# Small experts one at a time on both column halves, three fixed experts, an earlier ranking and another order at the end, in a mixer and grouped MoE layer

## Chip, cores and metric

One core of one Trainium2 chip. The time is device microseconds of one execution; the median of three runs of the kernel before is 969.6 (968.34 to 973.13). The profile is of one further execution. PE is TensorE, DVE VectorE, ACT ScalarE, POOL GpSimd, SP SyncE.

## What is computed

The layer has 1024 tokens of 1024 numbers, a token mixer (input projection, short convolution, pooling, spatial gating, output projection, LayerNorm), and then a mixture of 32 experts of which each token takes two:

```
h = x * (1 + scale2) + shift2
probs = softmax(h @ w_router + b_router)           # 32 experts in 4 groups of 8
g_sel = argmax over groups of the sum of the two best probs in the group
top_p, top_i = two best experts of that group ; weights = top_p / top_p.sum()
y[token] += weight * ((silu(xb @ w_gate[e]) * (xb @ w_up[e])) @ w_down[e])
x = LayerNorm(alpha * x + gate2 * y)
```

w_gate and w_up of an expert are 1024x512, w_down 512x1024, all fp32: 6 MB an expert, 192 MB in all, each read once. The tokens of an expert are some 26 to 130.

## The kernel before

**Mixer and routing.** Up to about 358 us the mixer runs in tiles of 128 tokens. Its last loop (over t) projects a tile, normalises it (`residual`), stores the row that the experts gather (`hrow`) and the base of the result (`acc_d`, both in DRAM), and routes it in three groups of tiles (`route_pick`, `route_place`, `route_list`). After the last group `ids` holds, for each expert, the tokens in its slots.

**Experts.** A work item is one big expert (a block of up to 128 tokens) or a pair of small ones (64 tokens each). The first four experts (`FIXED`) are processed as they are numbered, so that their weights can be loaded before routing is known. The other 28 are ranked by their count (`rank_experts`, `place_experts`): the largest gets two blocks (`DOUBLE`), the next eleven one block, the last sixteen 64 slots each, in eight pairs. `perm` holds the ranking; SP reads it (`expert`) before it issues a load of a ranked expert. A loop for overflowing experts runs at the end as often as `trip_i` says; it runs no time here.

**Chunks.** An expert's weights come in six chunks of 1 MB (gate and up in two each, down in two) into a ring of `NR` = 18 buffers, which also holds the split parts. A big expert's chunk is split into two parts of lower precision, wh (ACT, `split_tile`, L648) and wl (DVE, L653), and multiplied in three matmuls: wh with x_hi, wl with x_hi, wh with x_lo. A "whole" expert (the first one, and all small ones) is multiplied unsplit in fp32; each such matmul shows as two records in the trace. In a pair, the first expert's tokens are the 64 left stationary columns and the second's the 64 right ones, and each streams its own 512 weight columns (L1179, L1187).

**Order of work.** `chunks` lists the loads: up parts of an item, then the down parts of the item before. `Flow` counts buffers: `fill` issues loads while buffers are free, `take` splits, `parts_gone` frees the chunk that was used, takes ahead by `lead` chunks and fills up. A load is tied to the last matmul that has gone (`flow.last`). Every engine runs its instructions in the written order. `gather` fetches a block's rows into one of three buffers `xg` (POOL), `turn_part` transposes them, `swiglu` and `turn_h` make the hidden rows, `give` scales the output rows (L1232) and adds them to `acc_d` by an indirect accumulating DMA (L1234, POOL): one for a big block, two for a pair, 64 rows each. Scatters follow one another. Before the first block, three matmuls without use (`keep_warm`, L897) run on PE; the ranking and the sorting of the lists are small steps between the first two items' chunks (`steps_between`).

**End.** The last item is a pair; the down parts of a big expert and then of the pair come last. Then `acc_d` is read back and normalised (L1373 to L1405).

Of the kernel before, what the change touches and what calls it, by code (L numbers as in the profile page):

```python
# [38 lines left out]
AHEAD, FADE = 9, 12  # L39


@with_exitstack
def hybrid_trunk(ctx: ExitStack, tc: tile.TileContext, x, c, w_ada, b_ada, w_in, conv_w, conv_b,
# [48 lines left out]
    def load_rows():  # L92
        for r0, v in ((0, b_ada[0:2 * D].rearrange("(b p) -> b p", p=P)), (16, conv_w.rearrange("j (b p) -> (j b) p", p=P)),
# [25 lines left out]
                   allow_small_or_imprecise_dtypes=True)  # L119
    rcnt = const.tile([P, 2, 16], F32, name="rcnt")  # L120
# [23 lines left out]
    pw = const.tile([P, 2, P], F32, name="pw")  # L144
    nc.gpsimd.memset(pw, 0.0)
    wr = const.tile([P, KD, NE], F32, name="wr")
    br = const.tile([P, NE], F32, name="br")
    sgu = rt([P, 9, P], "sgu")
    wst, bs = sgu[:, 0:6], sgu[:, 6:9]
# [429 lines left out]

    xres = {}  # L580
# [5 lines left out]

    FIXED, BIG, DOUBLE, HALF = 4, 16, 4, P // 2
    PAIRS = (NE - BIG) // 2  # L590
    items = [(n,) for n in range(FIXED)]
    rest = [n for n in range(FIXED, BIG) if n != DOUBLE]
    rest.insert(1, DOUBLE)
    pairs = [(BIG + 2 * j, BIG + 2 * j + 1) for j in range(PAIRS)]
    for kind in "PBPBB" * 3 + "BPBBP":
        items.append((rest.pop(0),) if kind == "B" else pairs.pop(0))
# [10 lines left out]
    chunks, part_of = [], []  # L607
    for m in range(len(items) + 1):
        steps_ = [(w, h, m) for h in range(2) for w in (w_gate, w_up)] if m < len(items) else []
        steps_ += [(w_down, h, m - 1) for h in range(2)] if m else []  # L610
        for w, h, i in steps_:
            part = 1 + part_of[-1] if part_of else 0
            chunks += [(w, n, h) for n in items[i]]
            part_of += [part] * len(items[i])

    WHOLE = {items[0][0]} | set(range(BIG, NE))
    split_needed = [n not in WHOLE for _, n, _ in chunks]
# [243 lines left out]
    class Flow:  # L861
        taken, gone, used, others, lead, last = 0, 0, 0, 0, 2, None
# [18 lines left out]
    def parts_gone(last, n):  # L881
        flow.last = last
        for i in range(flow.gone, flow.gone + n):
            ready.pop(0)
            flow.used -= 1 + split_needed[i]
        flow.gone += n
        now = part_of[flow.gone] if flow.gone < len(chunks) else 0
        while (flow.taken < len(loaded) and part_of[flow.taken] - now < flow.lead and
               (not split_needed[flow.taken] or slots_used() + 1 < NR)):
            ready.append(take())  # L890
        fill(2)
# [6 lines left out]

    load_x(0)
    load_x(1)  # L900
    for t in range(NT):
# [32 lines left out]
        if t == NT - 1:  # L934

            flow.others = 3
# [5 lines left out]
    flow.others = 1  # L942
# [496 lines left out]
```

## Time and profile before

| | |
|---|---|
| median of 3 runs | 969.6 us |
| profiled execution | 968.15 us, its span 966.3 us |
| PE busy | 852.5 us (88%), 3992 instructions |
| DVE busy | 562.3 us (58%) |
| ACT busy | 364.3 us (38%) |
| POOL busy | 148.3 us (15%) |
| queue of loads (q1) | 258.25 MB, 68.3% of 16 DMA engines |
| software queue (q0: gathers, scatters, stores by POOL) | 26.60 MB, 9.7% |

The span is the time from the first to the last instruction of the profiled execution. Busy shares are means over the whole span; the stages have different limits, so they are read from windows. A matmul's end is modelled, so its duration overlaps the next one's; how fast matmuls follow each other is read from their starts.

### The profile page before, as it was taken

Reading aid. Unit: us, or ns where it says so; the run is one execution under the profiler, and the core shown is the slowest. Engines: PE = TensorE matmul, PEld = TensorE weight load, DVE = VectorE, ACT = ScalarE, POOL = GpSimd, SP = SyncE. Lnnn points to the kernel's source line nnn. Section 1 sums busy time; section 2 is a strip of 40 time slices with the busy share of each in tenths; the row PEclk is TensorE's granted clock in tenths of the full one; section 3 lists DMA queues with packets and bytes.
Section 4 is the critical chain, followed back from the end, with each engine's and each line's share of the span. In section 5 each row is a group of like instructions: output and inputs, shape, how many; then the busy total and the mean of one; then the engine's idle time right before and its main releaser. Section 6 shows DMA issues by size and latency. Waiting matters only on the chain. (4 is left out here: it accounts for less than half of the span.)

```text
span 966.3 us, 10876 instructions
## 1 busy us (share of the span) xinstructions
PE 852.5 (88%) x3992; PEld 584.2 (60%) x3992; DVE 562.3 (58%) x722; ACT 364.3 (38%) x401; POOL 148.3 (15%) x140
## 2 busy tenths in 40 slices
PE   3899999999799875999999999998999899899810
PEld 2778878877688752577555675565462657366400
DVE  6746844786667764687527356276170767266218
ACT  3453121124232333465515325065150655244207
POOL 0100000000000324222122131221211113111010
PEclk9999999999899997999999999999999999899975
DMA  9865163643444487189999999999999999999837
GB/s 302 286 211 227 71 191 109 218 153 111 194 174 153 166 320 312 44 323 377 417 404 414 398 366 393 394 416 407 391 409 396 412 402 384 381 382 413 330 93 279
DMA packets 77519, 285.58 MB, mean 296 GB/s; under 512 B 9852, under 2 KB 38856, under 8 KB 50840
## 3 DMA queue, kind: packets, MB, share of 16 engines
q1 hardware_dynamic: 66080, 258.25, 68.3%
q0 software_dynamic: 11296, 26.60, 9.7%
q8 instruction: 32, 0.52, 0.2%
q14 instruction: 23, 0.19, 0.1%
q10 hardware_dynamic: 88, 0.02, 0.0%
HBM read 268.79 MB, written 28.10 MB: 307 GB/s over the span
## 5 line engine op out<-in xcount | busy, mean ns | idle before, releaser
L653 DVE TENSOR_TENSOR wl<-w_raw,wh 128x2048 fp32r<-128x2048 f32 x90 | 204.4, 2288 | 109.4 <-ACT wh L648 104.9
L648 ACT ACTIVATE wh<-w_raw 128x2048 fp32r<-128x2048 f32 x90 | 171.1, 1914 | 108.8 <-DMA w_raw<-in_w_down_dram 65.4
L1179 PE MATMUL gu_ps<-w_raw,x_t 128*64 128x512 f32 (+1 forms) x544 | 139.8, 609 | 5.2 <-DMA w_raw<-in_w_up_dram 3.7
L1164 PE MATMUL gu_ps<-wh,x_hi 128*128 128x512 f32 x256 | 105.1, 410 | 0.0
L1165 PE MATMUL gu_ps<-wl,x_hi 128*128 128x512 f32 x256 | 100.8, 394 | 4.0 <-DVE wl L653 4.0
L1166 PE MATMUL gu_ps<-wh,x_lo 128*128 128x512 f32 x256 | 100.6, 393 | 0.0
L1179 PEld LDWEIGHTS gu_ps<-w_raw,x_t 128*64 128x64 f32 (+1 forms) x544 | 42.9, 142 | 79.0 <-issue 65.7
L295 PE MATMUL z_ps<-hh,w_hi 128*128 128x512 f32 x224 | 90.2, 403 | 0.0
L297 PE MATMUL z_ps<-hh,w_lo 128*128 128x512 f32 x224 | 87.3, 390 | 0.0
L296 PE MATMUL z_ps<-hl,w_hi 128*128 128x512 f32 x224 | 87.2, 389 | 0.0
L1187 PE MATMUL d_ps<-w_raw,m_ht 128*64 128x512 f32 (+1 forms) x272 | 63.8, 595 | 0.0
L1165 PEld LDWEIGHTS gu_ps<-wl,x_hi 128*128 128x128 f32 x256 | 48.2, 188 | 15.6 <-DVE wl L653 6.9
L1234 POOL DMA_INDIRECT acc_d<-m_o,place_ids x12 | 29.9, 2491 | 176.4 <-DVE m_o L1232 146.3
L1221 PE MATMUL d_ps<-wl,m_hl 128*128 128x512 f32 x128 | 51.7, 404 | 5.5 <-DVE wl L653 5.5
L669 PE MATMUL o_ps<-woh,y_lo 128*128 128x512 f32 x128 | 51.8, 404 | 5.4 <-DVE y_lo L466 5.4
L1220 PE MATMUL d_ps<-wh,m_hl 128*128 128x512 f32 x128 | 51.9, 405 | 4.3 <-ACT wh L648 4.3
L1164 PEld LDWEIGHTS gu_ps<-wh,x_hi 128*128 128x128 f32 x256 | 48.4, 189 | 12.0 <-issue 2.7
L1166 PEld LDWEIGHTS gu_ps<-wh,x_lo 128*128 128x128 f32 x256 | 48.1, 188 | 10.4
L667 PE MATMUL o_ps<-woh,y_hi 128*128 128x512 f32 x128 | 53.6, 419 | 0.0
L668 PE MATMUL o_ps<-wol,y_hi 128*128 128x512 f32 x128 | 51.5, 402 | 0.0
L1222 PE MATMUL d_ps<-wh,m_hl 128*128 128x512 f32 x128 | 51.1, 399 | 0.0
L295 PEld LDWEIGHTS z_ps<-hh,w_hi 128*128 128x128 f32 x224 | 42.1, 188 | 9.9 <-issue 1.4
(288 smaller groups left out, 1246.5 us busy)
## 6 DMA issues: line engine op xcount, KB each, us to landing
w_raw<-in_w_gate_dram SPq DMA_DIRECT2D x64, 1024.0 KB
w_raw<-in_w_up_dram SPq DMA_DIRECT2D x64, 1024.0 KB
w_raw<-in_w_down_dram SPq DMA_DIRECT2D x64, 1024.0 KB
ada_w<-in_w_ada_dram SPq DMA_DIRECT2D x16, 1024.0 KB
ada_w<-in_w_ada_dram SPq DMA_DIRECT2D x16, 512.0 KB
w_in<-in_w_in_dram SPq DMA_DIRECT2D x14, 512.0 KB
x_q<-in_x_dram SPq DMA_DIRECT2D x8, 512.0 KB
wo_raw<-in_w_out_dram SPq DMA_DIRECT2D x8, 512.0 KB
```

The lines of the kernel that those rows point to most:

```text
L295: nc.tensor.matmul(ps[:, h], wh, rhh, start=k == 0, stop=False)
L296: nc.tensor.matmul(ps[:, h], wh, rhl, start=False, stop=False)
L297: nc.tensor.matmul(ps[:, h], wl, rhh, start=False, stop=k == KD - 1)
L648: nc.scalar.activation(wh, w, AF.Copy)
L653: nc.vector.tensor_sub(wl, w, wh.bitcast(F32))
L667: nc.tensor.matmul(ps[:, h], hi[:, k], wh, start=k == 0, stop=False)
L1164: nc.tensor.matmul(ps[:, m], hi[:, k], wh[:, o], start=k == 0, stop=False)
L1165: nc.tensor.matmul(ps[:, m], hi[:, k], wl[:, o], start=False, stop=False)
L1166: last = nc.tensor.matmul(ps[:, m], lo[:, k], wh[:, o], start=False, stop=k == KD - 1)
L1179: last = nc.tensor.matmul(ps[sl, m], xt[:, k, sl], w[:, o], start=k == 0, stop=k == KD - 1)
L1187: last = nc.tensor.matmul(ps[sl, h], ht[:, k, sl], w[:, o], start=k == 0, stop=k == KF - 1)
L1220: nc.tensor.matmul(ps[:, h], hi[:, k], wh[:, o], start=k == 0, stop=False)
```

## The change

It has four parts. (1) Three experts are fixed instead of four, and none of them is whole. Of the first one, three chunks are split before routing ends: ACT makes three wh ahead of the token lists; the three wl, the ranking and the placing stand between the gather's issue and the first block. Tie-breaking constants are made earlier. 14 chunks are loaded before that instead of 18. (2) Small experts are items of their own: the same 64 tokens stand in both column halves, the left half streams 256 of a chunk's 512 columns, the right half the other 256; in the down part the halves stream the two halves of the 1024 output columns. The output has 64 rows of each half and is added with one scatter of 128 half rows. (3) The items come as B B B, S S, then B S alternating thirteen times, then S (B big, S small). (4) Before the last item, the down part of the item before it is loaded and used ahead of the last item's up part.

```diff
+FIXED, BIG, DOUBLE, HALF = 3, 16, 3, P // 2
+SMALL = NE - BIG
...
-    for kind in "PBPBB" * 3 + "BPBBP":
-        items.append((rest.pop(0),) if kind == "B" else pairs.pop(0))
+    rest.insert(3, DOUBLE)
+    for kind in "SS" + "BS" * 13 + "S":
+        items.append((rest if kind == "B" else small_).pop(0))
...
+        up = [(w, items[m], h) for h in range(2) for w in (w_gate, w_up)] if m < len(items) else []
+        dn = [(w_down, items[m - 1], h) for h in range(2)] if m else []
+        chunks += dn + up if m == len(items) - 1 else up + dn
-    WHOLE = {items[0][0]} | set(range(BIG, NE))
-    split_needed = [n not in WHOLE for _, n, _ in chunks]
+    split_needed = [n < BIG for _, n, _ in chunks]
...
-            flow.others = 3
+            flow.others = 3 + FIRST + 1
...
+    nc.scalar.activation(xg[2], g2row, AF.Copy, scale=0.0)
+    flow.others = 0
+    first = [take(True) for _ in range(FIRST)]
+    for g in xg[:2]:
         nc.scalar.activation(g, g2row, AF.Copy, scale=0.0)
     route_place(GROUPS[-1])
     route_list(GROUPS[-1])
...
-    def gate_up_whole(e, ps, k, m, parts):
-        xt, = xs[e]
+    def gate_up_half(e, ps, k, m, part):
+        xt = xs[e]
+        w, = part
         for k in range(k, k + 4):
-            o = slice((k % 4) * 512, (k % 4 + 1) * 512)
-            for sl, (w,) in columns(parts):
-                last = nc.tensor.matmul(ps[sl, m], xt[:, k, sl], w[:, o], start=k == 0, stop=k == KD - 1)
+            cols = by_row(w[:, (k % 4) * 512:(k % 4 + 1) * 512], KF)
+            for i, sl in enumerate(SIDES):
+                last = nc.tensor.matmul(ps[sl, m, 0:2 * P].rearrange("q (a p) -> q a p", a=2), xt[:, k],
+                                        cols[:, 2 * i:2 * i + 2], start=k == 0, stop=k == KD - 1)
+    def down_half(ht, ps, i, part):
+        w, = part
+        for a in range(2):
+            for j, sl in enumerate(SIDES):
+                last = nc.tensor.matmul(ps[sl, 0], ht[:, a, SIDES[i]], w[:, a * D + j * 512:a * D + j * 512 + 512],
+                                        start=a + i == 0, stop=a + i == 2)
...
+    def give_half(ps, n):
+        o = qt([P, D // 2], "m_o")
+        nc.vector.scalar_tensor_tensor(o, ps[:, 0], half_wts[:, n:n + 1], g2half, op0=OP.mult, op1=OP.mult)
+        add_rows(o, half_ids[:, n:n + 1], acc_d.rearrange("s (h n) -> (s h) n", h=2))
...
-    gather(upper_ids[:, 0:1], xg[2])
-    keep_warm(3)
+    gather(nothing, xg[2])
+    ranks, lists = rank_counts(), []
+    keep_warm(1)
     gather_to(3)
+    first[0][1]()
+    ranks = rank_experts(*ranks)
+    first[1][1]()
+    place_experts(*ranks)
+    keep_warm(1)
+    first[2][1]()
     for g in range(2):
         turn_blocks(0, g)
-    ready += [take() for _ in range(2)]
+    ready += [w for w, _ in first]
+    fill(0)
...
+        if not nxt:
+            flow.lead = 4
+            down(done, [turn_h(b) for b in done])
+        for i in range(4):
+            gate_up(i)
+            small_step(i)
+            if i == 0 and m and nxt:
+                turned = [turn_h(b) for b in done]
+            if i in (1, 2) and nxt:
+                turn_blocks(m + 1, i - 1)
+        gather_to(sum(b[0] <= m + 1 for b in seq) + 3)
```

`first[i][1]()` is the wl subtraction of a chunk whose wh is made already; `cols` takes every fourth column of a chunk's row (two interleaved sets for each half), so that the hidden rows fit the layout of w_down.

The instructions move at three places. First DVE between the cast of `ids` and the first block. Before, the ranking starts at once behind the cast (key, rank, onto, diag are its steps):

```order
L845 CAST ids<-ids_f 128x32
L996 COPY ranking<-cnt_ps 128x32
L998 SCALAR_TENSOR_TENSOR ranking<-ranking 128x32
L1000 MEMSET ranking 128x1 x4
L1002 SCALAR_TENSOR_TENSOR k_keyc<-cnt_ps,tie_c 32x1
L1003 SCALAR_TENSOR_TENSOR k_keyc<-eid_c,k_keyc 32x1
L1005 TENSOR_SCALAR k_own<-eid_c 32x1
L1007 TENSOR_SCALAR k_top<-eid_c 32x1
L1008 SCALAR_TENSOR_TENSOR k_keyc<-k_own,k_top,k_keyc 32x1
L1011 SCALAR_TENSOR_TENSOR ranking,k_rank<-ranking,k_keyc,ones 32x32
```

Now, from the last steps of the ranking to the first block's x_lo (one more wl, of the first chunk, stands right behind the cast):

```order
L1012 TENSOR_SCALAR ranking<-ranking,col 32x32
L1013 TENSOR_SCALAR ranking<-ident,k_rank 32x32
L663 TENSOR_TENSOR wl<-w_raw,wh 128x2048
L1020 CAST perm<-perm_ps 128x32
L1022 TENSOR_SCALAR o_at<-perm_ps 128x1
L1024 TENSOR_SCALAR left<-perm_ps 128x32
L1026 TENSOR_SCALAR ranking<-perm_ps 128x32
L1027 SCALAR_TENSOR_TENSOR left<-left,ranking 128x32
L1028 TENSOR_TENSOR left<-ranking,left 128x32
L663 TENSOR_TENSOR wl<-w_raw,wh 128x2048
L1148 TENSOR_TENSOR x_lo<-xg_ps,x_hi 128x512 x2
```

Three wl, the ranking and the placing now stand ahead of the x_lo of the first block; before, the first block had no x_lo.

Second PE in the middle of the expert stage. Before, a pair's up parts between two big experts (mh_ps transposes h, xg_ps the next block):

```order
L1179 MATMUL gu_ps<-w_raw,x_t 64x512 x8
L1203 MATMUL mh_ps<-ident,m_gh 128x128 x4
L1179 MATMUL gu_ps<-w_raw,x_t 64x512 x8
L1151 MATMUL xg_ps<-ident,xg_2682 128x128 x4
L1179 MATMUL gu_ps<-w_raw,x_t 64x512 x8
```

Now, a small expert behind a big one, with the down part of the small one before it ahead:

```order
L1178 MATMUL d_ps<-w_raw,m_ht 64x512 x8
L1170 MATMUL gu_ps<-w_raw,x_t 64x256 x8
L1202 MATMUL mh_ps<-ident,m_gh 128x128 x4
L1170 MATMUL gu_ps<-w_raw,x_t 64x256 x8
L1144 MATMUL xg_ps<-ident,xg_2684 128x128 x4
L1170 MATMUL gu_ps<-w_raw,x_t 64x256 x8
```

A chunk of one expert is now eight matmuls of 256 columns; before, two chunks of two experts were eight of 512.

Third PE at the end, up to the read of `trip_i`. Before, the last pair's up parts are followed by 24 matmuls of a big expert's down part, of which the first three stand here, with the pair's h transposed in their middle, and then by 16 matmuls of the pair's down part (L1187):

```order
L1179 MATMUL gu_ps<-w_raw,x_t 64x512 x8
L1203 MATMUL mh_ps<-ident,m_gh 128x128 x4
L1179 MATMUL gu_ps<-w_raw,x_t 64x512 x24
L1220 MATMUL d_ps<-wh,m_hl 128x512
L1221 MATMUL d_ps<-wl,m_hl 128x512
L1222 MATMUL d_ps<-wh,m_hl 128x512
```

Now:

```order
L1217 MATMUL d_ps<-wh,m_hl 128x512
L1197 MATMUL mh_ps<-ident,m_gh 128x128 x2
L1178 MATMUL d_ps<-w_raw,m_ht 64x512 x8
L1170 MATMUL gu_ps<-w_raw,x_t 64x256 x32
L1197 MATMUL mh_ps<-ident,m_gh 128x128 x2
L1178 MATMUL d_ps<-w_raw,m_ht 64x512 x8
```

The last eight chunks are those of small experts, unsplit, and the last down part is of one expert.

## Rows read from the trace of the kernel before

**Rows 1.** The page's strip of moved GB/s, in 40 slices of 24.2 us

```profile
GB/s 302 286 211 227 71 191 109 218 153 111 194 174 153 166 320 312 44 323 377 417 404 414 398 366 393 394 416 407 391 409 396 412 402 384 381 382 413 330 93 279
```

**Rows 2.** Stretches: length, busy time of each engine, granted clock, DMA share, GB/s

```profile
382.00:407.00 25.00, 22.67 (x78) 12.63 (x78) 14.75 (x38) 10.69 (x10) 10.18 (x15) 1.00 0.06 15
407.00:422.00 15.00, 15.00 (x58) 9.39 (x56) 7.73 (x21) 5.79 (x6) 0.10 (x1) 1.00 0.95 377
422.00:427.00 5.00, 5.00 (x26) 4.17 (x25) 4.97 (x3) 4.40 (x4) 0.00 (x0) 1.00 0.40 107
430.00:911.00 481.00, 458.06 (x2056) 283.24 (x2054) 251.88 (x170) 201.13 (x169) 97.01 (x50) 0.99 1.01 397
911.00:923.00 12.00, 10.65 (x49) 4.87 (x48) 2.63 (x4) 0.60 (x1) 1.57 (x1) 1.00 0.39 123
923.00:936.00 13.00, 0.00 (x0) 0.00 (x0) 1.12 (x1) 0.00 (x0) 2.98 (x2) 0.70 0.16 21
936.00:966.30 30.30, 0.00 (x0) 0.00 (x0) 22.65 (x29) 19.61 (x37) 0.00 (x0) 0.50 0.73 278
```

**Rows 3.** Timeline of SP around the gap in the loads: start, duration, instruction

```profile
364.20 0.33 SPq L637 DMA_DIRECT2D w_raw<-in_w_up_dram  x1
407.28 0.33 SPq L637 DMA_DIRECT2D w_raw<-in_w_gate_dram  x1
```

**Rows 4.** Timeline of PE and DVE, from the token lists to the first items

```profile
375.40 4.37 PE L897 MATMUL warm_ps<-g2row,ident 128*128 128x512 f32 x6
375.90 0.18 DVE L845 CAST ids<-ids_f 128x32 int32<-128x32 f32 x1
382.32 3.70 PE L1179 MATMUL gu_ps<-w_raw,x_t 128*128 128x512 f32 x8 [0.24 <-issue]
386.18 0.19 DVE L996 COPY ranking<-cnt_ps 128x32 f32<-128x32 f32 x1 [10.10 <-PE gu_ps L1179]
388.31 0.22 DVE L1015 TENSOR_SCALAR ranking<-ident,k_rank 32x32 f32<-32x32 f32 x1
389.87 2.29 DVE L653 TENSOR_TENSOR wl<-w_raw,wh 128x2048 fp32r<-128x2048 f32 x1 [1.34 <-issue]
408.48 0.69 DVE L1157 TENSOR_TENSOR x_lo<-xg_ps,x_hi 128x512 fp32r<-128x512 f32 x1 [0.80 <-ACT x_hi L1153]
```

**Rows 5.** Timeline of PE: two big experts, then a pair

```profile
424.16 0.63 PE L1203 MATMUL mh_ps<-ident,m_gh 128*128 128x128 f32 x4
441.97 0.63 PE L1203 MATMUL mh_ps<-ident,m_gh 128*128 128x128 f32 x4
457.15 3.65 PE L1179 MATMUL gu_ps<-w_raw,x_t 128*64 128x512 f32 x16
460.74 0.75 PE L1203 MATMUL mh_ps<-ident,m_gh 128*128 128x128 f32 x4
461.42 3.65 PE L1179 MATMUL gu_ps<-w_raw,x_t 128*64 128x512 f32 x16
491.52 7.09 PE L1187 MATMUL d_ps<-w_raw,m_ht 128*64 128x512 f32 x32
```

**Rows 6.** Timeline of PE in the mixer, and groups of weight loads by line and shape

```profile
195.43 1.97 PE L376 MATMUL mix_ps<-sgu,vn 128*64 128x128 f32 x32
L1151 PEld LDWEIGHTS xg_ps<-ident,xg 128*128 128x128 f32 x200 | 27.8, 191 | 21.5 <-issue 12.8 <-DVE m_hl L1211 3.3 <-DVE x_lo L1157 2.9
L355 PEld LDWEIGHTS v_ps<-ident,v 128*128 128x128 f32 x24 | 3.1, 140 | 1.3 <-ACT v L448 0.2 <-ACT vn L361 0.2
```

**Rows 7.** Timeline of DVE, POOL and SP at the end of the expert stage

```profile
922.83 1.28 DVE L1232 SCALAR_TENSOR_TENSOR m_o<-d_ps,pair_wts,g2row 128x1024 f32<-128x1024 f32 x1 [5.75 <-PE d_ps L1187]
924.39 1.42 POOL L1234 DMA_INDIRECT acc_d<-m_o,pair_ids  x1 [5.46 <-DVEq L1350]
928.94 1.56 POOL L1234 DMA_INDIRECT acc_d<-m_o,upper_ids  x1 [3.12 <-DMA acc_d<-m_o,pair_ids]
935.98 4.93 SPq L1373 DMA_DIRECT2D z<-acc_d  x8
```

More of the change, by code (lines that the diff above doesn't have):

```diff
@@ L578, in hybrid_trunk @@
         split_wo(k)
+    tie_breaks()
     xres = {}
@@ L879, in fill, with chunk_gone @@
             load_chunk(queue)
-    def parts_gone(last, n):
+    def chunk_gone(last):
         flow.last = last
[L883 to L888, printed above, removed]
+        ready.pop(0)
+        flow.used -= 1 + split_needed[flow.gone]
+        flow.gone += 1
+        while (flow.taken < len(loaded) and flow.taken - flow.gone < flow.lead and
                (not split_needed[flow.taken] or slots_used() + 1 < NR)):
@@ L1142, in turn_part @@
     def turn_part(e, src, g):
[L1144 removed]
+        if is_half(e):
+            if g == 0:
+                xt = xs[e] = qt([P, KD, HALF], "x_t")
+                ps = tp("xg_ps")
+                for j in range(KD):
+                    nc.tensor.transpose(ps[:, j * HALF:(j + 1) * HALF], by_row(src, KD)[0:HALF, j], ident[0:HALF, 0:HALF])
+                nc.scalar.activation(xt.rearrange("p a b -> p (a b)"), ps, AF.Copy)
+            return
         if g == 0:
[L1146 to L1147 removed]
+            xs[e] = qt([P, KD, P], "x_hi", F32R), qt([P, KD, P], "x_lo", F32R)
         hi = xs[e][0]
@@ L1299, in gate_up, with down @@
                     swiglu(b, p)
-            parts_gone(last, len(parts))
-        def down(blocks, turned, between=None):
-            it = items[blocks[0][0]]
-            whole = is_whole(blocks[0])
+            chunk_gone(last)
+        def down(blocks, turned):
             po = [zp("d_ps") for _ in blocks]
+            half = is_half(blocks[0])
             for i in range(2):
-                parts = ready[:len(it)]
                 for p, v in zip(po, turned):
-                    last = down_whole(v, p, i, parts) if whole else down_part(v, p, i, parts[0])
-                if i == 0 and between:
-                    between()
-                parts_gone(last, len(parts))
+                    last = (down_half if half else down_part)(v, p, i, ready[0])
+                chunk_gone(last)
             for b, p in zip(blocks, po):
-                give(p, weights(b), scattered(b))
+                if half:
+                    give_half(p, items[b[0]] - BIG)
+                else:
+                    give(p, weights(b), slots(b))
         def small_step(i):
```

218 lines of the change are left out of this document (82 added, 136 removed).

## The prediction

> **What bounds the kernel now.** I read the page's strip of bandwidth first [rows 1]: from slice 18 of 40 on, the DMA engines move some 400 GB/s in nearly every slice, with one hole (44 GB/s) at about 386 to 411 us and a fall at the end. So I cut the expert stage into stretches [rows 2]. Between 430 and 911 us the DMA share is 1.01 at 397 GB/s while PE is busy 458 of 481 us: DMA sets the pace, PE is close behind. Ahead of it lies the hole: 25 us (382 to 407) at 15 GB/s, later 5 us at 107 GB/s. Behind it come 12 us in which PE finishes, 13 us in which only the last scatters run, and 30.3 us of final LayerNorm. Three things can therefore change the time: when the stream of weights resumes, how long its bytes take, and what follows the last byte. The queue of loads [rows 3] says why the hole is there: the 18th load is issued at 364.20, the next at 407.28. All 18 buffers hold raw chunks, and each fixed expert behind the first needs a net buffer more for its split, so the buffers that the first expert frees go to splits and not to loads.
>
> **Part 1: three first chunks split early, ranking in the gap, three fixed experts.** By the order, only 14 chunks are loaded before the first block, a 15th once the first split is done, and the 16th once the third chunk has been used; from there each chunk used admits one load. The first block now waits on VectorE: behind the cast of `ids`, which ends at 376.1 [rows 4], stand three wl subtractions (2.29 each, 6.9), the ranking (2.35 from the first row to the last in the old form, of which seven small operations go: 1.6 left), the placing (six operations of some 0.2: 1.2), and x_lo (0.69): 386.5. In the kernel before, the first matmul ran at 382.32 and no x_lo was needed. From 386.5 ten of a chunk's twelve matmuls end the first chunk at 389.0 (a chunk takes 2.97, see below). Two warm-up matmuls stand where three stood, with waits between; in the old stretch a warm-up record took 0.73 us (4.37 over 6) against 0.46 in the block behind it (3.70 over 8) [rows 4], so the first chunk may run partly at the lower of the two clocks: up to 2.5 us more. I take 390; the ends are 385 (nothing waited for) and 394.
>
> A big expert takes PE 17.8 us, from one transposition of h (424.16) to the next (441.97) [rows 5], 2.97 a chunk. The third chunk is thus used at 396, and the 16th load goes out then, 11 us before the old 19th. Three loads fewer are in by that time, 3 x 1.0486 MB at 397 GB/s, 7.9 us: the net gain here is some 3 us, plus the second dip (5 us at 107 GB/s lose 3.7).
>
> **Part 2: bytes.** By 430 us some 24 loads had landed before (18, and 5.7 + 0.5 MB of the two stretches behind 407 [rows 2] with the first microseconds of the next), so the 191.0 MB of 430 to 911 (481 x 397) are 168 loads, 176.2 MB, and 14.8 MB of gathers and scatters. Rows whose index is out of bounds are not moved, so 64-row gathers and half-row scatters carry the same bytes. From 396 on there remain 177 loads and some 16.3 MB of indirect traffic: 201.9 MB, at 397 GB/s 508.6 us, so 904.6. In the first three experts loads are let in one per 2.97 us, near the pace of the stream itself (2.64 for a load alone at 397 GB/s), and the lists are still sorted there; I add 3 us: last weights at **908** (before 911).
>
> **Part 3: small experts.** Before, a pair's gate and up parts take 3.59 us for 16 records (8 matmuls, two records each: 457.15 to 460.74), 0.224 a record of 512 columns, and its down 7.09 for 32 [rows 5]. Now a chunk of one expert is again 16 records of 64 stationary columns, of 256 moving ones. The nearest rows: 32 records of the same halves with 128 columns take 1.97 us, 0.062 each [rows 6], and 0.224 at 512; between them 0.116 at 256, 1.86 a chunk. So a small expert costs 4 x 1.86, its down 3.55 (half of 7.09) and three groups of transpositions among half-array matmuls at 0.68 (460.74 to 461.42): 13.0 us. PE in all: 17 blocks x 17.8 and 16 x 13.0, 511 us, from 387 (390 less one chunk) to 898, against weights until 908. DMA stays the bound, with only 10 us to spare.
>
> One thing about these matmuls the trace does not show: their moving operand steps by 4 elements (16 bytes). The nearest row is a load of stationary columns: 128 of them with a step of 8 elements (xg_ps) take 191 ns, contiguous ones (v_ps) 140 [rows 6], 51 ns dearer. Nothing excludes a gain, but no row promises one, so the low end is 0; at the high end the same 0.4 ns a column falls on every moving column, 102 ns on each record of 116. I take 0: a half's stream asks for a column only every 0.88 ns (2 x 0.224 us for 512), twice the 0.4 ns that the step added to a loaded one, so it should fit into the pace. [...]
>
> **Part 4: the end.** Before, from 911 on: a split, half of a big expert's down, a pair's down, the output op at 922.83, two scatters of which the second waits for the first (924.39, 928.94), the reads at 935.98 [rows 7]: 25 us. Now the last eight chunks are unsplit ones of two small experts, one scatter follows. From 908: one down chunk 1.8, the output op on half the columns 0.7 (of 1.28), 0.3 to POOL, the scatter between 4.55 (first to second) and 7.04 (second to the reads), I take 5.8: **916.6**; the LayerNorm's 30.3 us [rows 2] give a span of 947. The last ln2 loads stay where they were in the queue.
>
> **What else moves, at no cost.** The tie breaks (POOL and four tiny VectorE operations) stand ahead of the projection, off any wait; the pair shift goes away; the pool weights in another buffer change nothing that waits. POOL issues as many scatters (33) and eight more gathers; it sat idle 384 us of 481 [rows 2]. If that cover went (a gather behind a scatter that waits), the next block's transpositions would be late by a scatter, some 5 us.
>
> **The sum.** Part 1 and 2: 911 to 908. Part 4: 25 us to 8.6. Span 966.3 to 947. The profiled run took 968.15 with a span of 966.3, so 1.85 lie around it, and the median of the runs is 969.6, 1.45 above it: 947 + 1.85 + 1.45 = **950 us**.
>
> **Rivals.**
> *Strided columns make PE the bound (slower).* If the step costs half of its high end, 51 ns a record, a gate or up chunk takes 2.67 and a small expert 16.3; PE needs 302.6 + 260 = 563 us, from 387 to 950, the span is 950 + 0.7 + 0.3 + 5.8 + 30.3 = 987, the time **990**; at the full 102 ns it is 1042, and so too if the two halves did not run side by side. It decides from 30 ns a record on: then PE ends at 929 and the span is the old one. For it: the 191 against 140 ns, and the thin spare. Against: the pace argument, and that halves of 128 columns do overlap [rows 6]. Chance 0.20.
> *VectorE becomes the bound in the first three experts.* Six splits (13.7), two x_lo, m_hl, m_gh at 0.69 and the output 1.28 come to 17.8 us an expert, just PE's 17.8, and now all three are split and the lists are sorted there. If PE loses 8 us, loads are let in that much later: **958**. For it: five microseconds at 422 to 427 had VectorE busy 4.97 [rows 2]. Against: three splits are done ahead. Chance 0.14.
> *Small experts stall between their chunks.* Their chunks are half as long, so the transposed blocks (two PSUM buffers, emptied by ScalarE and VectorE behind splits of 1.9 and 2.29 us) may come late. At 1.8 us an expert PE ends at 927, the span is 963: **967**, no change. For it: four transpositions between half-array chunks already take 0.68. Against: PE has 10 us to spare before any of it counts. Chance 0.08.
>
> **How the numbers follow.** The forecast, within 6 us of 950, has 0.58. A measurement of this kernel can tell about 0.5% (5 us) from no change. Faster by over that: forecast and second rival, 0.72; same 0.08; slower 0.20. The range: 944 (first chunk at 385, a scatter of 4.55) to 980, which takes in the second and third rivals and a step cost of up to 42 ns; what is left out above is most of the slower cases, below little.
>
> **What would show it.** In the changed profile the first third matmul of a block (wh with x_lo) should run near 386.5; the load behind the 15th near 396; GB/s from there near 397 without a hole; records of 64x256 every 0.116 us; PE idle some 10 us in the stage; last weights near 908; one scatter, reads at about 917. It would be wrong if gate/up chunks of small experts took over 2.3 us, if DMA fell under 385 GB/s for long with PE full, or if the first block started after 394.

## The result and the profile after

The changed kernel takes **1071.2 us** (median of 4 runs, 1069.4 to 1075.4) where the kernel before took 969.1 beside it (4 runs): a ratio of 1.105, 95% interval 1.1003 to 1.1097. I had forecast 950, with 944 to 980 as the range. The profiled execution took 1069.4 with a span of 1067.6.

The page's strip of bandwidth of the changed kernel (26.7 us a slice; before: [rows 1]):

```profile
GB/s 304 229 275 122 188 50 197 182 134 217 177 139 208 285 92 264 333 399 310 348 363 338 295 262 204 382 308 324 344 353 343 367 359 322 376 346 334 306 35 291
```

Before, it stood at some 400 from slice 19 to 37. Now it lies mostly between 300 and 360: the DMA no longer sets the pace. The same in stretches (length, busy time of PE, PEld, DVE, ACT, POOL, then granted clock, DMA share, GB/s), to hold against [rows 2]:

```profile
366.00:380.00 14.00, 7.97 (x36) 4.29 (x37) 13.41 (x54) 6.93 (x6) 7.59 (x4) 0.50 0.14 33
380.00:396.00 16.00, 12.18 (x43) 9.17 (x42) 8.13 (x11) 8.23 (x8) 11.55 (x14) 0.71 0.28 96
411.00:430.00 19.00, 18.88 (x78) 15.10 (x77) 11.24 (x20) 10.13 (x8) 2.38 (x3) 0.85 0.67 231
445.00:980.50 535.50, 534.75 (x2421) 304.35 (x2420) 247.22 (x175) 192.72 (x175) 92.12 (x54) 1.00 0.93 334
1006.50:1036.70 30.20, 22.18 (x98) 7.32 (x98) 3.02 (x4) 1.15 (x3) 4.69 (x3) 0.97 0.26 70
```

From 445 to 980 PE is busy 534.75 of 535.5 us, and the DMA has fallen to 334 GB/s. PE is the bound. The hole in the loads has not gone but moved ahead (33 GB/s from 366 to 380, 96 from 380 to 396, since 14 chunks are in and not 18), only 231 GB/s flow between 411 and 430, and PE still has 22 us of work and the scatters another 8 behind 1006.5. What PE does, in its timeline around one small expert and the down of the one before it (start, duration, instruction):

```profile
578.00 3.65 PE L1178 MATMUL d_ps<-w_raw,m_ht 128*64 128x512 f32 x16
581.49 3.80 PE L1170 MATMUL gu_ps<-w_raw,x_t 128*64 128x256 f32 x16
585.22 0.74 PE L1202 MATMUL mh_ps<-ident,m_gh 128*128 128x128 f32 x4
```

Held against the pair of [rows 5]: the down of one small expert takes 3.49 us (578.00 to 581.49), half of the pair's 7.09, as forecast. A gate or up chunk takes 3.73 (581.49 to 585.22), though its records have half the columns of the pair's, which took 3.59. That is 0.233 us a record where I had put 0.116. There are 64 such chunks: 64 x (3.73 - 1.86) = 120 us more on PE.

The start of the stage, PE (what it waited for stands in brackets) and VectorE, to hold against [rows 4]:

```profile
381.40 0.79 PE L1157 MATMUL gu_ps<-wh,x_lo 128*128 128x512 f32 x1
388.83 0.40 PE L1055 MATMUL ls_ps<-ranking 32*128 32x32 f32 x2 [1.43 <-DVE ranking L1047]
391.62 0.60 PE L1056 MATMUL ls_ps<-ranking 32*128 32x16 f32 x2 [2.39 <-DVE ranking L1053]
410.81 0.37 PE L1045 MATMUL lt_ps<-ident,ranking 128*32 128x128 f32 x1 [4.11 <-DVE ranking L1277]
412.26 0.63 PE L1156 MATMUL gu_ps<-wl,x_hi 128*128 128x512 f32 x1
412.68 0.63 PE L1157 MATMUL gu_ps<-wh,x_lo 128*128 128x512 f32 x1
```

```profile
371.81 0.18 DVE L855 CAST ids<-ids_f 128x32 int32<-128x32 f32 x1
386.29 2.29 DVE L663 TENSOR_TENSOR wl<-w_raw,wh 128x2048 fp32r<-128x2048 f32 x1 [4.35 <-ACT wh L658]
388.50 0.27 DVE L1047 COPY ranking<-lt_ps 32x128 f32<-32x128 f32 x1
389.15 2.29 DVE L663 TENSOR_TENSOR wl<-w_raw,wh 128x2048 fp32r<-128x2048 f32 x1 [0.37 <-ACT wh L658]
391.36 0.21 DVE L1053 COPY ranking<-ranking 32x128 f32<-32x128 f32 x1
408.29 2.28 DVE L663 TENSOR_TENSOR wl<-w_raw,wh 128x2048 fp32r<-128x2048 f32 x1
410.48 0.18 DVE L1277 COPY ranking<-tab 128x32 f32<-128x32 f32 x1
```

This execution reached the lists some 4 us earlier than the profiled one of before (`ids` cast at 371.81 against 375.90). From the end of that cast (371.99) to the first matmul with x_lo (381.40) it took 9.4 us; I had forecast 10.4. Then comes what I had allowed 3 us for: the list steps need matmuls on PE, whose inputs are tiny VectorE copies, and these copies stand in VectorE's queue behind wl subtractions of 2.29 us, the first of which had itself waited 4.35 us for ScalarE's wh. PE waits 1.43, 2.39 and 4.11 us for the copies. After the last of these its records come 0.42 us apart (412.26, 412.68): the granted clock was 0.50 from 412 to 416, and also from 392 to 396, behind the second wait.

### The profile page after: what moved, and what is told of

The parts are those of the page before. It is cut to its first block, busy times and chain, and to the rows that moved or that the text cites. A ratio compares the mean times of both kernels' runs of the same rounds, so it can differ in the third digit from the quotient of the medians.

```text
span 1067.6 us, 12238 instructions
## 1 busy us (share of the span) xinstructions
PE 976.6 (91%) x4590; PEld 635.0 (59%) x4590; DVE 583.6 (55%) x738; ACT 376.4 (35%) x425; POOL 160.2 (15%) x150
## 3 DMA queue, kind: packets, MB, share of 16 engines
q0 software_dynamic: 11936, 26.60, 9.4%
## 4 chain that ended last, share of the span: by engine, by line
PE 81%; DVE 9%; another core or an unknown queue 3%; ACT 2%; DMA 2%; issue 1%; SPq 0%; DVEq 0%; ACTq 0%; POOLq 0%
PE gu_ps L1170 21%; PE gu_ps L1155 6%; PE gu_ps L1156 6%; PE gu_ps L1157 6%; PE z_ps L315 5%; PE z_ps L316 5%; PE z_ps L317 5%; PE d_ps L1178 4%; PE d_ps L1215 3%; PE d_ps L1216 3%; PE d_ps L1217 3%; PE xg_ps L1144 2%; PE o_ps L677 2%; PE o_ps L679 2%; PE o_ps L678 2%
## 5 line engine op out<-in xcount | busy, mean ns | idle before, releaser
L663 DVE TENSOR_TENSOR wl<-w_raw,wh 128x2048 fp32r<-128x2048 f32 x96 | 217.9, 2289 | 64.1 <-ACT wh L658 59.9
L1170 PE MATMUL gu_ps<-w_raw,x_t 128*64 128x256 f32 x1024 | 243.0, 632 | 0.0
L658 ACT ACTIVATE wh<-w_raw 128x2048 fp32r<-128x2048 f32 x96 | 179.4, 1906 | 14.1 <-PE gu_ps L1156 8.5
L1170 PEld LDWEIGHTS gu_ps<-w_raw,x_t 128*64 128x64 f32 x1024 | 75.1, 150 | 129.3 <-issue 124.3
L1157 PE MATMUL gu_ps<-wh,x_lo 128*128 128x512 f32 x272 | 108.1, 398 | 0.0
L1189 DVE TENSOR_TENSOR m_gh<-m_gh,gu_ps 128x512 f32<-128x512 f32 (+1 forms) x33 | 18.4, 559 | 154.2 <-ACT m_gh L1188 154.2
L1221 POOL DMA_INDIRECT acc_d<-m_o,place_ids x13 | 40.1, 3083 | 189.4 <-DVE m_o L1227 189.4
L1188 ACT ACTIVATE m_gh<-gu_ps 128x512 f32<-128x512 f32 (+1 forms) x33 | 16.3, 494 | 145.4 <-PE gu_ps L1157 76.1
L1178 PE MATMUL d_ps<-w_raw,m_ht 128*64 128x512 f32 x256 | 58.4, 598 | 0.9 <-ACT m_ht L1199 0.9
L1123 POOL DMA_INDIRECT xg<-hrow,place_ids x29 | 31.7, 1093 | 138.5 <-PE xg_ps L1144 123.4
```

Source lines behind the costliest of these rows:

```text
L658: nc.scalar.activation(wh, w, AF.Copy)
L663: nc.vector.tensor_sub(wl, w, wh.bitcast(F32))
L1157: last = nc.tensor.matmul(ps[:, m], lo[:, k], wh[:, o], start=False, stop=k == KD - 1)
L1170: last = nc.tensor.matmul(ps[sl, m, 0:2 * P].rearrange("q (a p) -> q a p", a=2), xt[:, k], cols[:, 2 * i:2 * i + 2], start=k == 0, stop=k ...
L1178: last = nc.tensor.matmul(ps[sl, 0], ht[:, a, SIDES[i]], w[:, a * D + j * 512:a * D + j * 512 + 512], start=a + i == 0, stop=a + i == 2)
```

## The experiments

Two theories stood at first. **Step:** the 16-byte step of the moving operand doubles what each column takes. **Sharing:** two halves of one expert do not run side by side, because they share a chunk and the stationary columns, or because 256 columns are too short. Both fit 0.233 us a record. Every time below is a median of 4 to 12 runs, but for three kernels that ran once, as is said with each; the kernel before took 969.3 to 970.9 beside these runs.

**Contiguous columns.**

```diff
-            cols = by_row(w[:, (k % 4) * 512:(k % 4 + 1) * 512], KF)
...
-                                        cols[:, 2 * i:2 * i + 2], start=k == 0, stop=k == KD - 1)
+                                        w[:, o + 2 * P * i:o + 2 * P * (i + 1)], start=k == 0, stop=k == KD - 1)
...
-            for j in range(2):
-                nc.tensor.transpose(ps[:, j * P:(j + 1) * P], h[:, j * P:(j + 1) * P], ident)
+            for j in range(KF):
+                for sl in SIDES:
+                    nc.tensor.matmul(ps[sl, j * HALF:(j + 1) * HALF], by_a[:, j], ident[:, sl], start=True, stop=True)
```

> The changed kernel, but each column half of a small expert reads 256 neighbouring columns of the chunk instead of columns 16 bytes apart; the hidden rows are put back in order by eight small transpositions instead of two large ones. Same records, same loads. Step theory (the 16-byte step of the moving operand doubles its time): a gate or up chunk of a small expert falls from 3.75 us to about 1.9, the DMA becomes the bound again at some 390 GB/s, and the time is 950 to 965 us. Sharing theory (two halves of one expert do not run side by side, since they share the chunk and the stationary columns, or because 256 columns are too short): the chunk stays at 3.75 and the time at 1071. Other parts of the change are to blame: chunk 1.9, time still above 990.

995.0 us, ratio to before 1.025 (1.021 to 1.028). PE's timeline of the contiguous version around a small expert:

```profile
563.21 1.90 PE L1170 MATMUL gu_ps<-w_raw,x_t 128*64 128x256 f32 x16
565.03 0.75 PE L1204 MATMUL mh_ps<-ident,m_gh 128*128 128x128 f32 x4
```

A chunk takes 1.82 (563.21 to 565.03): the size I had forecast, with the same records and the same sharing of chunk and stationary columns. The sharing theory is out, and the step is worth 76 of the 102 us. That is less than the 120 us of PE, since the DMA is the bound again: from 440 to 890 its share is 1.00 at 378 GB/s. But 25 us remain above the kernel before: the 950 to 965 of the first clause were missed, and the third clause holds too.

**Other steps, one side alone.** The matmuls of each chunk read

```diff
-                                        cols[:, 2 * i:2 * i + 2], start=k == 0, stop=k == KD - 1)
+                    last = nc.tensor.matmul(out[i], xt[:, k], flat1[:, i], **go[i])
...
+                    last = nc.tensor.matmul(out[i], xt[:, k], by2[:, i], **go[i])
...
+                    last = nc.tensor.matmul(one[0], xt[:, k], flat1[:, i], **go1[i])
...
+                    last = nc.tensor.matmul(one[0], xt[:, k], by4[:, 2 * i:2 * i + 2], **go1[i])
```

> The changed kernel with another moving operand in each of a small expert's four gate and up chunks (its results for small experts are no longer the layer's): first chunk step 1 element, both halves; second chunk step 2 elements (8 bytes), both halves; third chunk step 1, all matmuls on the lower half alone; fourth chunk step 4 elements, lower half alone. Step theory, paid by each column: 1.9, between 1.9 and 3.7, 3.6, 7.2 us for the 16 records. Step theory, paid where the two halves read together (one read path for both): 1.9, 1.9 to 3.7, 3.6, 3.6. Sharing theory: 3.7, 3.7, 3.6, 3.6.

PE's timeline of one small expert, the four chunks in this order:

```profile
583.16 1.90 PE L1178 MATMUL gu_ps<-w_raw,x_t 128*64 128x256 f32 x16
585.66 2.04 PE L1181 MATMUL gu_ps<-w_raw,x_t 128*64 128x256 f32 x16
588.71 3.67 PE L1184 MATMUL gu_ps<-w_raw,x_t 128*64 128x256 f32 x16
593.40 7.41 PE L1187 MATMUL gu_ps<-w_raw,x_t 128*64 128x256 f32 x16
```

1.9, 2.0, 3.7, 7.4 (one run, 1071.2; the four chunks together take some 15 us, as they did in the changed kernel): each column pays, on each half by itself, and the halves still run side by side. Eight bytes cost next to nothing (2.04 against 1.90), sixteen double the time (7.41 against 3.67).

> The changed kernel, results not the layer's: a small expert's gate and up chunks use step 8 elements (32 bytes, both halves), then runs of two neighbouring elements every 16 bytes (both halves), then step 2 on the lower half alone, then runs of two on the lower half alone. A big expert's four chunks, split fp32r over the full array, use step 1, step 2, step 4, and runs of two every 16 bytes. [...] Step theory, price grows with the distance: 7.4 for step 8. Sharing theory: 3.7 in every small chunk, and 2.7 in every chunk of a big expert.

The edit is of the same kind in the small chunks, and in the big ones

```diff
-            nc.tensor.matmul(ps[:, m], hi[:, k], wh[:, o], start=k == 0, stop=False)
+                h_, l_ = (w.rearrange("p (n s) -> p s n", s=4)[:, j] for w in part)
+                nc.tensor.matmul(ps[:, m], hi[:, k], h_, **go)
...
```

A small expert's chunks in PE's timeline (step 8, runs of two, step 2 on one half, runs of two on one half), then matmuls of a big one with step 1, with step 2 and with step 4:

```profile
621.82 3.85 PE L1199 MATMUL gu_ps<-w_raw,x_t 128*64 128x256 f32 x16
626.27 2.04 PE L1202 MATMUL gu_ps<-w_raw,x_t 128*64 128x256 f32 x16
629.32 3.82 PE L1205 MATMUL gu_ps<-w_raw,x_t 128*64 128x256 f32 x16
634.16 3.82 PE L1208 MATMUL gu_ps<-w_raw,x_t 128*64 128x256 f32 x16
...
643.51 0.39 PE L1160 MATMUL gu_ps<-wh,x_hi 128*128 128x512 f32 x1
643.73 0.39 PE L1161 MATMUL gu_ps<-wl,x_hi 128*128 128x512 f32 x1
...
649.58 0.65 PE L1166 MATMUL gu_ps<-wl,x_hi 128*128 128x512 f32 x1
650.04 0.65 PE L1167 MATMUL gu_ps<-wh,x_lo 128*128 128x512 f32 x1
...
661.64 0.64 PE L1171 MATMUL gu_ps<-wl,x_hi 128*128 128x512 f32 x1
662.10 0.65 PE L1172 MATMUL gu_ps<-wh,x_lo 128*128 128x512 f32 x1
```

A chunk with a step of thirty-two bytes takes 3.8 us, as with one of sixteen, so the price does not grow with the distance (one run, 1178.6). Two neighbouring columns of every sixteen bytes are nearly free (2.04 against 1.90, and 3.82 against 3.67 on one half). In the big experts, which read fp32r over the full array, any step I tried doubles the time: 0.22 us from record to record at step 1, 0.46 at steps 2 and 4 (runs of two showed the same mean, 0.63 us a record against 0.39). Records at a granted clock of 0.50 look alike (0.63 us, 0.42 apart, in the start of the changed kernel), so the granted clock has to be read beside it (the number ahead of the DMA share):

```profile
649.00:661.00 12.00, 12.00 (x35) 5.84 (x33) 1.39 (x1) 0.38 (x1) 2.88 (x1) 1.00 0.45 129
663.00:665.00 2.00, 2.00 (x6) 1.38 (x5) 0.00 (x0) 0.00 (x0) 0.00 (x0) 0.50 0.94 371
```

At step 2 it was 1.00 throughout, so the doubling is the step's. And at step 4 records came 0.46 us apart also while it was 0.50 (663.48, 663.94): the pace of this stepped stream did not follow the clock.

**The step alone, in the kernel before.**

```diff
-                last = nc.tensor.matmul(ps[sl, m], xt[:, k, sl], w[:, o], start=k == 0, stop=k == KD - 1)
+                last = nc.tensor.matmul(ps[sl, m].rearrange("q (a p) -> q a p", a=KF), xt[:, k, sl],
+                                        by_row(w[:, o], KF), start=k == 0, stop=k == KD - 1)
...
```

> The kernel before, in which only the moving operand of the gate and up matmuls of the pairs and of the unsplit first expert steps by 4 elements (512 columns, 16 bytes apart), the hidden columns coming out already in the order that the transpositions want. Step theory: the 16 records of a pair's gate or up part go from 3.6 us to about 7.2; 32 such parts and 4 of the first expert add some 120 us to PE, whose spare was 23 us in 430 to 911, so about 1060 to 1075 us. Sharing theory: halves belong to two experts with chunks of their own, so nothing changes: 969 us.

1066.8 us (one run); a pair's part goes from 3.65 to 7.41:

```profile
477.12 7.41 PE L1179 MATMUL gu_ps<-w_raw,x_t 128*64 128x512 f32 x16
```

The step suffices to make the kernel before about as slow as the changed one.

**The remaining 25 us: start, end, or small experts one at a time.** The lists first:

```diff
             if i == 3:
                 for b, p in zip(now, ps):
                     swiglu(b, p)
+            small_step(i)
             chunk_gone(last)
...
```

> The contiguous version, in which the list steps of the first two experts are issued ahead of the next splits, so that on VectorE they no longer stand behind one or two wl subtractions of 2.29 us. Theory that the start costs the contiguous version its time (PE there waits 1.44, 2.38 and 4.11 us for the lists and then runs a dozen records at half the clock twice, so buffers come free some 10 us late): faster by 5 to 12 us, 983 to 990. Theory that the small experts' PE time and the stage as a whole set the end, whatever the start does: within 3 us of 995.

984.5 us, 10.5 less than the contiguous version: the start theory, at its upper end. PE's waits in its start were 4.1, 3.2 and 1.4 us for the lists (by line); now:

```profile
PE lt_ps L1045 <- DVE ranking L1279: 2.6, 1, 2.6
PE ls_ps L1056 <- DVE ranking L1053: 1.0, 1, 1.0
```

The 16th load went out 11.6 us behind the 15th, where it had been 17.2. The end in the old order:

```diff
-        chunks += dn + up if m == len(items) - 1 else up + dn
+        chunks += up + dn
...
```

> The contiguous version with the end in the old order: the gate and up of the last small expert ahead of the down of the one before it. My forecast counted 16.7 us for the shorter end, so by it the old end costs up to 16 us more: 1005 to 1012. Theory that PE is behind the weights at the end, and the same matmuls run in either order: within 3 us of 995.

996.2: no difference. The new order at the end is worth nothing. The start alone, in the kernel before with its pairs, and then with the lists first:

```diff
-    FIXED, BIG, DOUBLE, HALF = 4, 16, 4, P // 2
+FIXED, BIG, DOUBLE, HALF = 3, 16, 3, P // 2
...
-    WHOLE = {items[0][0]} | set(range(BIG, NE))
+    WHOLE = set(range(BIG, NE))
...
+    first = [take(True) for _ in range(FIRST)]
...
```

> The kernel before with its pairs and its end, and only the start changed: three fixed experts, all split, three splits ahead of the first block, ranking and placing between them, 14 chunks loaded ahead, lists sorted behind the first chunks. My forecast gave this part a gain of about 3 us: 966. Theory that the start loses bytes (3.98 GB/s-slices against 4.35 in the 140 us around the first block of the contiguous version, 3.7 MB, 9 us at 397 GB/s): 976 to 982. If the start is no part of the loss: 966 to 972, and the 25 us of the contiguous version are those of small experts one at a time.

> The kernel before with only the start changed, as in the run ahead of it, and the list steps ahead of the next splits on VectorE. Start theory: 5 to 12 us faster than that run. Otherwise within 3 us of it. If below 965, it beats both kernels.

973.2 (ratio 1.003, 1.0008 to 1.0052) and 973.5 (1.0027, 1.0005 to 1.0049). The start alone costs 0.3%, hardly more than can be told from no change: 973 lies between the 966 to 972 of no loss and the theory's 976 to 982, and neither held, nor did my gain of 3 us. The lists bring nothing here, where the sort has one copy less in front of it and PE waited 1.4 us once ahead of the 16th load, not 1.4 and 2.4. So with equal starts (984.5 against 973.5) small experts one at a time, free of the step, still lose 11 us to pairs (with their order of items, their end and their eight small transpositions).

**Is it PE's sum?**

```diff
+            if k % 2:
+                continue
             for i, sl in enumerate(SIDES):
...
```

> The contiguous version with the lists first, in which the small experts leave out every second matmul of gate and up (loads, gathers, transpositions and downs as before; their results are not the layer's). Some 16 x 3.7 = 59 us... at most 58 us less on PE. Theory that PE's sum is what the small experts one at a time lose (their 13.1 us each against 23.5 for a pair, 21 us over all): well below 984.5, to 968 or less. Theory that the loads run slower with them (order of the items, half-row scatters): stays within 4 us of 984.5.

990.0 us (983.1 to 990.7): nothing gained, if anything 5 us lost. The same stretch, 440 to 890, of the kernel before, of the contiguous version with the lists first, and of this run:

```profile
440.00:890.00 450.00, 429.73 (x1938) 266.39 (x1938) 237.38 (x160) 188.84 (x160) 92.56 (x47) 0.99 1.01 398
```

```profile
440.00:890.00 450.00, 435.66 (x2535) 299.04 (x2533) 229.40 (x166) 183.20 (x167) 100.67 (x53) 0.99 1.00 379
```

```profile
440.00:890.00 450.00, 404.68 (x2088) 278.08 (x2087) 227.88 (x166) 182.11 (x165) 91.60 (x53) 0.94 1.01 379
```

PE has become idle by 45 us of 450, and the DMA, busy without a break in all three, moves 379 GB/s in the last two and 398 in the first. PE's sum was not it. The DMA carries the same bytes more slowly.

**Runs of two: the change repaired.**

```diff
-            cols = by_row(w[:, (k % 4) * 512:(k % 4 + 1) * 512], KF)
+            cols = w[:, (k % 4) * 512:(k % 4 + 1) * 512].rearrange("p (n j a) -> p j n a", j=2, a=2)
...
```

(with the lists first, and the transposition of h reading every second column)

> The changed kernel with the lists first, in which a half reads two neighbouring columns of every 16 bytes (its hidden columns are pairs, and the two large transpositions of h read every second of them). By the runs at other steps a record then takes what a contiguous one does, 0.117 us spacing, 1.9 a chunk. Two transpositions instead of eight small ones save some 0.8 us for each small expert, 13 us of PE. Theory that PE's sum counts: 974 to 981. Theory of the loads: 984 as the contiguous version with the lists first. If runs of two cost anything here: above 990.

981.7, between the two clauses: the two large transpositions stay, and with them it is 3 us faster than the contiguous one. A chunk takes 2.03 us; in 440 to 890 the DMA moves 382 GB/s.

```profile
517.75 2.03 PE L1170 MATMUL gu_ps<-w_raw,x_t 128*64 128x256 f32 x16
```

**Why the DMA is slower.** Five kernels changed one thing each in this repaired version, a sixth in the kernel before:

```diff
-    for kind in "SS" + "BS" * 13 + "S":
+    for kind in "B" + "SSBSSBB" * 3 + "BSSBBSS":
...
```

> The repaired change (runs of two, lists first; 981.7 us, 381 GB/s from 440 to 910), in the old order of the items: two small ones where a pair stood (B, then SS B SS BB three times, B SS BB SS behind the fixed experts). If the order of the items (splits spread evenly, B and S in turn) slows the loads: back to 393 to 397 GB/s and 970 to 975. If not: 381 GB/s and 979 to 985.

988.1 (981.7 to 993.3), 378 GB/s: not the order of the items.

```diff
-AHEAD, FADE = 9, 12
+AHEAD, FADE = 14, 12
```

> The repaired change with up to 14 chunks let in ahead of use to the end of the stage instead of a bound that falls from 18 to 9. If too few loads are on their way (the DMA engines' packets take longer with fewer queued): 390 GB/s or more and 970 to 976. If depth does not matter: within 3 us of 981.7; if later splits find no buffers: slower.

985.4, 384 GB/s: not the number of loads on their way.

```diff
-        add_rows(o, half_ids[:, n:n + 1], acc_d.rearrange("s (h n) -> (s h) n", h=2))
```

> The repaired change without the scatters of the small experts (their results are not added; 16 scatters of 1024 KB... of 64 whole rows' bytes, some 3 MB, fall away). If the half-row scatters slow the loads beyond their own bytes: 393 to 397 GB/s, and with the last scatter gone from the end 962 to 970. If they cost only their bytes (3 MB, 8 us of DMA time) and the last one 6 us: 968 to 976 at some 381 GB/s for what is left.

963.0, 387 GB/s. The whole execution moves 2.9 MB less, 7.6 us at 382 GB/s, and the end from the last issue of weights to the reads of z shrinks from 28.9 to 20.8 us; together they make the 18.7 gained but for 3.

```diff
-            gather(slots(seq[sent[0]]), xg[sent[0] % 3])
+            if not is_half(seq[sent[0]]):
+                gather(slots(seq[sent[0]]), xg[sent[0] % 3])
```

> The repaired change (runs of two, lists first: 981.7 us; 382 GB/s from 440 to 890) without the gathers of the small experts, which work on whatever rows lie in the buffer (their results are not the layer's; some 3.8 MB fall away). If the 64-row gathers slow the loads: 393 GB/s or more for what is left, 960 to 966. If they cost only their bytes (3.8 MB at 380 GB/s, 10 us): 970 to 974 at 380 GB/s.

969.5, 390 GB/s, again with 2.9 MB less (7.6 us) for 12.2 gained.

```profile
440.00:890.00 450.00, 441.35 (x2430) 301.56 (x2430) 243.19 (x175) 194.13 (x176) 84.33 (x41) 1.00 1.00 390
```

PE is busy 441 of 450 us in it. The gathers cost somewhat more than their bytes, but they do not bring back 396.

```diff
+        if m < len(items) and items[m] >= BIG:
+            up = [up[i] for i in (0, 2, 1, 3)]
...
```

> The repaired change, in which a small expert's chunks come as both halves of gate, then both halves of up, instead of gate and up in turn. If neighbouring loads matter (pairs load the same matrix of two experts one behind the other): 388 to 396 GB/s and 970 to 977. If not: within 3 us of 981.7, 380 to 383 GB/s.

> The kernel before with the chunks of every item as both halves of gate, then both halves of up. If neighbouring loads matter, its 398 GB/s (440 to 890) rise to 405 or more and it takes 958 to 964, less than both kernels; if not, 966 to 972; PE's accumulation and swiglu are the same work in another order.

986.0 at 382 GB/s, and 969.7 at 396: which loads stand side by side does not matter. (988.1, 985.4 and 986.0 lie 4 to 6 us above 981.7, more than the expectations gave a change without effect; their rates stay within 4 GB/s of 382.)

The traces narrow the loss down. The queue of loads in 440 to 890 (packets, MB, share of 16 engines), in the kernel before, in the repaired one, and in that without the small experts' scatters and without their gathers:

```profile
q1 hardware_dynamic: 22684, 165.19, 88.9%
q1 hardware_dynamic: 21714, 158.13, 87.9%
q1 hardware_dynamic: 22353, 162.78, 90.8%
q1 hardware_dynamic: 22483, 163.69, 89.2%
```

The share of 16 engines over 450 us, divided by the packets, gives the time of one packet: 282, 291, 292 and 286 ns. It is 282 to 285 in every version with pairs and contiguous columns, and 291 to 293 in every one with small experts one at a time, their gathers and no 16-byte step. So most of the 4% lies in the loads' own packets, and most of that goes with the gathers of the small experts, not with their scatters. What makes the packets slower **stays open**: in the changed kernel, where PE sets the pace, one takes 307 ns, so more than the gathers can lengthen it, and a version without both gathers and scatters was not run.

**The end of the kernel before.** The same edit in two kernels:

```diff
-    for kind in "PBPBB" * 3 + "BPBBP":
+    for kind in "PBPBB" * 3 + "BPBPB":
```

> The kernel before, only the last two items exchanged: the pair ahead of the last big expert, so that the stage ends on one scatter instead of two that wait for each other. If the end is set by the last weights and what follows them: behind them stand one split (some 2 + 2.29 us), a quarter to a half of a down, the output op 1.28 and one scatter of some 6, about 13 us instead of 25, so 10 to 12 us faster: 957 to 961. If PE is behind there with more than that, 2 to 6 us faster (the second scatter alone, 4.55): 965 to 969.

> The kernel before with the changed start, the lists first and the last two items exchanged. If the exchange gains what it gains in the kernel before, this is as much below 973.5: 960 to 964 by the end theory, 968 to 971 otherwise.

979.5, ten us slower than before, where either clause had it faster, and 973.1, no change. POOL's timeline at the end of the first, where the pair's first scatter went out at 925.84:

```profile
930.53 1.57 POOL L1234 DMA_INDIRECT acc_d<-m_o,upper_ids  x1 [3.27 <-DMA acc_d<-m_o,pair_ids]
935.67 1.56 POOL L1234 DMA_INDIRECT acc_d<-m_o,place_ids  x1 [3.57 <-DMA acc_d<-m_o,upper_ids]
```

The pair's two scatters now stand just ahead of the last one, and all three wait for each other (3.27 and 3.57 us). But in the second kernel they stand in the same chain and the time does not move, so this is not shown to be the reason. No version that keeps the whole computation beat the kernel before.

## Why the prediction was wrong

**The step that failed: "I take 0".** Part 3 named the 16-byte step, bounded it from 0 to 102 ns a record, and took the low end by an argument on pace: a half asks for a column only every 0.88 ns, and 0.4 ns fits into that. One half alone shows the pace: 16 records in 3.67 us at step 1, 0.90 ns a column, and 7.41 at step 4, 1.81 ns. The extra does not hide behind the pace, it is the pace once more; in the changed kernel 0.233 - 0.114 = 119 ns a record, above my high end. That end came from loads of stationary columns, 191 ns with a step (xg_ps) against 140 without (v_ps). That the 51 ns are the step's was my estimate: in the same trace the loads of x_hi (L1164), which have no step, took 189. The moving stream's step doubled its time. The first rival had the mechanism, 0.20 of the chances, and 990 to 1042; with 119 ns its own working gives 16 x 4 x 1.90 = 122 us on PE over the forecast, PE done at 1020, and 1060. Two of my signs of being wrong came with it: chunks over 2.3 us (3.73), and the DMA under 385 GB/s with PE full (334).

The small experts' chunks show the price at each step: 3.80 us with one column in every 16 bytes and 3.85 with one in every 32, 2.04 with two neighbours in every 16 bytes and with every second column, 1.90 contiguous. The big experts' fp32r matmuls do not agree: with two neighbours in every 16 bytes a record still took 0.63 us against 0.39. The argument on pace was an estimate that no row showed, and I should have given the first rival more than 0.20.

**Part 1, the start: right in its own term, short of the lists.** x_lo came 9.4 us behind the cast, not 10.4. The 16th load I had at 396, 20 us behind the cast of `ids`; it was issued 17 us behind the 15th, near 397.6, some 26 behind the cast. Between stand two waits of PE (1.43 and 2.39 us) for lists that queue behind wl subtractions on VectorE, and a stretch at a granted clock of 0.50 (392 to 396); the third wait (4.11) and another such stretch (412 to 416) hold back the 20th, which goes out at 417.08, ten us behind the 19th. For all of this the forecast had the 3 us that Part 2 adds for the lists. The second rival had VectorE as the bound of the first three experts, but by its sum, not by the order in its queue; issuing the list steps ahead of the splits gave 10.5 us (contiguous version). My text asked what is queued behind a waiting instruction for the ranking, and not for the list steps that come next.

**Part 2, the bytes: wrong by a rate.** 201.9 MB at 397 GB/s was the old stage's rate. With small experts one at a time the DMA, fully busy, moves 378 to 384: 201.9 MB then take 526 to 534 us, not 509. The bytes were the same, 26.60 MB on the software queue in both kernels; the small experts' scatters moved 2.89 MB of them (23.71 MB are left without them), where all their half rows would be 4.19, so rows out of bounds were not moved. But "the same bytes" did not mean the same time.

**Part 3 but for the step: right.** Contiguous chunks take 1.82 (1.86), a down 3.49 (3.55).

**Part 4, the end: its own stretch nearly right, the gain half of what I had.** I forecast 8.6 us from the last weights to the reads of z, in place of 25. SyncE's timeline of the repaired version:

```profile
916.74 4.76 SPq L647 DMA_DIRECT2D w_raw<-in_w_down_dram  x2
...
950.36 4.42 SPq L1366 DMA_DIRECT2D z<-acc_d  x8
```

The row holds two issues, the second at its end, 921.50. By the packets of the trace the last weights land at 939.6, and the reads follow 10.7 us behind. But in the kernel before the last weights land at 916.7, not at 911, where the rate only begins to fall: from there to the reads at 935.98 [rows 7] it is 19.2 us, not 25. So the end shrinks by 8.5 us where I had 16.4. Counted from the last issue it is 35.5 us before (900.49 to 935.98) and 28.9 in the repaired version; the contiguous one has 30.2 with the new order and 28.9 with the old. The small experts shorten the end, the order does not. In the changed kernel it is 33.9, since PE has 22 us of work left behind 1006.5, which I had counted as used up as the weights arrive.

**The account.** Of the 102 us, taken off in this order, 76 are the step (1071.2 to 995.0), 10.5 the lists behind the splits (to 984.5), 11 small experts one at a time, with the lower DMA rate (to 973.5), and 3 to 4 are left for the start, about what a measurement can tell. The parts hold in this order alone: with pairs, the lists first gained nothing.

## What to carry to other kernels

An operand that steps is priced by what its own kind of matmul takes alone: put two steps side by side in one run before building on it, and where a layout forces a step, keep two neighbouring elements in every 16 bytes if the matmul is fp32 on a half of the array (here 2.04 us a chunk instead of 3.80). When a stage moves to another engine's queue, list what stands ahead of each small instruction that a matmul waits for. A rate read from a saturated stage belongs to that stage's pattern of transfers, and a new pattern of the same bytes needs a margin (here 398 GB/s became 382, 4%).

## What the runs showed of the hardware that I had not expected

Two kinds of matmul differ: an fp32 matmul on half the array reads columns 8 bytes apart at no cost to speak of (2.04 against 1.90 us a chunk), while an fp32r matmul over the full array takes twice as long at the same step (0.46 against 0.22 us from record to record), and with runs of two; whether the type or the half array makes the difference was not tried. At step 4 the fp32r records kept their 0.46 us when the granted clock fell to 0.50. A busy DMA is not one rate: at a share of 1.00 to 1.01 it moved 378 to 398 GB/s in versions of one kernel. And less work on PE can leave the time where it was: half of the small experts' gate and up matmuls left out gave 990 against 984.5 us, PE idle 45 us of 450 and its granted clock at 0.94.
